# Attention of the first block: products with the values on column halves, transposed, and the division moved to the gate

## The chip, the cores and the metric

The kernel runs on one core of a Trainium2 chip. The metric is the device time of one execution in microseconds. The profile and the trace are of one further execution.

## The reference, cut to what matters

Two transformer blocks run one after the other over 256 tokens of width 1024. The first has two layers. Each mixes four branches of width 256 (attention, a convolution, a Fourier mix, a gated unit), multiplies them by a gate and projects the result out:

```
s = jnp.einsum("bqhd,bkhd->bhqk", q, k) * scale
pr = jax.nn.softmax(s, axis=-1)
attn = jnp.einsum("bhqk,bkhd->bqhd", pr, v)
...
y = jnp.concatenate([attn, conv, four, sgu], axis=-1) * jax.nn.silu(hp[..., GATE_OFF:])
return y @ p["w_out"]
```

The attention has four heads with values of width 64. In layer 0 the 256 tokens of `x` attend to 512 keys (x and context), and the 256 context tokens to the 256 context keys. In layer 1 only `x` has queries. The second block has two layers of feed-forward, token mixer, feed-forward; it reads the first block's output.

## The kernel before

Tokens are tiled by 128: tiles 0 and 1 are `x`, 2 and 3 the context. All products that need it are made in three passes: each float32 weight tile is streamed by SyncE (SP) into a `raw` buffer (`Stream.fetch`, L330), ScalarE (ACT) casts it to `whi`, VectorE (DVE) subtracts to get `wlo`, and TensorE (PE) multiplies high and low parts. `raw` has few slots, shared with the chunks `ada` of the matrix from which shift, scale and gate come. DVE multiplies each such chunk with the conditioning vector and sums it (`adaj`). So a DMA starts when DVE has let a buffer go, and PE's next weights wait for DMA, ACT and DVE in turn.

The order of each engine's instructions is fixed when the program is built: a planner in Python (`Sched`) keeps a clock per engine, adds an estimated cost per operation (`act` L216, `dve` L221, `mm` L230, `transpose` L234), and runs side jobs (`spawn`, generators that yield the time or the event they wait for) when they fall due. All instructions thus show the planner's lines, and their names tell them apart.

`First.attend` (L1621) handles one tile and one layer. For each head: scores `sc` on PE, the row maximum `mx` on DVE, `p` = exp on ACT with the row sums in `den`, transposes `tpp` of `p` in blocks of 128 keys, a copy to `pT` on ACT, the reciprocal `rd` on DVE. Then one matmul per key block, with `pT` as the 128x128 weights and 128 columns of `V` moving, which are two heads:

```
S.mm(ch, 0.218, av[:, :P], pT[:, j * P:(j + 1) * P],
     v[:, 2 * c:2 * c + 2, :].rearrange("p h d -> p (h d)"), start=j == 0, stop=j == nb - 1)
S.act(ch, 64, "mul", o[:, h * 64:(h + 1) * 64], av[:, b * 64:(b + 1) * 64], rd[:, h:h + 1], x=0.09)
```

Half of each result is not used. ACT divides the other half by the row sum into `att`. A tile has 4 key blocks (tiles 0 and 1) or 2 (tiles 2 and 3), so 16 or 8 such matmuls.

`put` (L1307) joins a branch and its gate. Whichever comes first is written to `y`, the second multiplies it on DVE. Branch 0 is the attention. For four of six tiles the attention came first and ACT copies it (`y<-att`), and the gate comes as a factor `fac`; for two the gate came first. Then `y_out` transposes `y` on PE (`tpy`), ACT makes the high part of `yT` and DVE the low part, and the output product `yo` uses them. The rest that the prediction names: `acc` (the convolution's 31 taps on DVE), `tpc<-acc` (its result transposed back), `ln` (its layernorm), `tpc<-ln` and `pw` (its pointwise product).

Of the kernel before, what the change touches and what calls it, by code (L numbers as in the profile page):

```python
# [8 lines left out]
F32 = mybir.dt.float32  # L9
F32R = mybir.dt.float32r  # L10
I32 = mybir.dt.int32
AF = mybir.ActivationFunctionType
ALU = mybir.AluOpType
PSUM = bass.MemoryType.PSUM
P = 128
# [135 lines left out]
class Event:  # L151
    def __init__(self):
        self.at = None
# [805 lines left out]
class Layer:  # L959


    def __init__(self):
        self.F, self.V, self.kT, self.qT, self.sgm, self.y, self.yT = {}, {}, {}, {}, {}, {}, {}


class First:
# [337 lines left out]
        S.act(ch, 256, "activation", z, src, AF.Identity, scale=r, bias=b, x=0.15)  # L1304
        return z

    def put(self, t, b, ch, emit=None, val=None):  # L1307

        S, l = self.S, self.l[t]
        L, key = self.L[l], (l, t, b)  # L1310
        T, i = (4, t) if l == 0 else (2, t % 2)
        if b not in L.y:
            L.y[b] = self.s4([P, T, 256], f"y{b}")
        dst = L.y[b][:, i, :]
        if key not in self.ystate:
            self.ystate[key] = ch
            if emit:
                emit(dst)
            else:
                S.act(ch, 256, "copy", dst, val)  # L1320
            return
        if emit:
            val = self.w2([P, 256], "fac")
            emit(val)
        ch.t = max(ch.t, self.ystate[key].t)
        S.dve(ch, 256, "tensor_tensor", dst, dst, val, op=ALU.mult)
        S.spawn(self.y_out(t, b, ch))

    def part(self, l, b, n):
        return self.L[l].yT[b][n] if l == 0 else self.L[l].yT[b][:, n]  # L1330

    def y_out(self, t, b, ch):
        S = self.S
        yield ch
        l = self.l[t]
        T, i = (4, t) if l == 0 else (2, t % 2)
        if b not in self.L[l].yT:
            self.L[l].yT[b] = [self.s4([P, 2, T, P], f"yT{b}{n}", F32R) for n in range(2)] if l == 0 else \
                self.s4([P, 2, 2, T, P], f"yT{b}", F32R)
        hi, lo = (self.part(l, b, n)[:, :, i, :] for n in range(2))  # L1340
        tp = self.psum("tp", "tpy")
        for c in range(2):
            self.tr(ch, tp[:, c * P:(c + 1) * P], self.L[l].y[b][:, i, c * P:(c + 1) * P])
        src = tp[:, :256].rearrange("p (c t) -> p c t", c=2)
        S.act(ch, 256, "copy", hi, src)
        S.dve(ch, 256, "tensor_sub", lo, src, hi.bitcast(F32))
        S.done(self.L[l].yev[t][b], ch)
# [273 lines left out]
    def attend(self, t, l):  # L1621

        S, L = self.S, self.L[l]
        s, i = divmod(t, 2)
        keys = (0, 1) if s == 0 else (1,)
        yield L.ev["mla", t]
        for k in keys:
            for j in range(2):
                yield L.ev["mla", 2 * k + j]
        nk = 256 * len(keys)  # L1630
        nb = nk // P
        den = self.small.tile([P, 4], F32, tag="den1", name="den1", bufs=4)
        rd = self.small.tile([P, 4], F32, tag="rd1", name="rd1", bufs=4)
        o = self.w2([P, 256], "att")
        for h in range(4):
            ps = self.psum("ps", "sc1")
            ch = S.chain()
            for n, k in enumerate(keys):
                S.mm(ch, 0.432, ps[:, n * 256:(n + 1) * 256], L.qT[s][:, h, i * P:(i + 1) * P], L.kT[k][:, h, :],
                     start=True, stop=True)  # L1640
            mx = self.small.tile([P, 1], F32, tag="mx1", name="mx1", bufs=4)
            S.dve(ch, nk, "tensor_reduce", mx, ps[:, :nk], axis=mybir.AxisListType.X, op=ALU.max, negate=True)
            p = self.w2([P, 512], "p1")
            S.act(ch, nk, "activation", p[:, :nk], ps[:, :nk], AF.Exp, bias=mx, accum_out=den[:, h:h + 1], x=0.19)
            yield ch
            tp = self.psum("tp", "tpp1")
            for j in range(nb):
                self.tr(ch, tp[:, j * P:(j + 1) * P], p[:, j * P:(j + 1) * P])
            pT = self.w2([P, 512], "pT1")
            S.act(ch, nk, "copy", pT[:, :nk], tp[:, :nk])  # L1650
            S.dve(Chain(ch.t), 16, "reciprocal", rd[:, h:h + 1], den[:, h:h + 1])
            yield ch
            av = self.psum("tp", "av1")
            c, b = divmod(h, 2)
            for j in range(nb):
                v = L.V[2 * keys[j // 2] + j % 2]
                S.mm(ch, 0.218, av[:, :P], pT[:, j * P:(j + 1) * P],
                     v[:, 2 * c:2 * c + 2, :].rearrange("p h d -> p (h d)"), start=j == 0, stop=j == nb - 1)
            S.act(ch, 64, "mul", o[:, h * 64:(h + 1) * 64], av[:, b * 64:(b + 1) * 64], rd[:, h:h + 1], x=0.09)
        self.put(t, 0, ch, val=o)  # L1660


    def weight(self, t):
# [33 lines left out]
    def begin(self, l):  # L1697

        if l in self.L:
            return  # L1700
        L = self.L[l] = Layer()
        L.c = self.layer_consts(l)
        L.ev = {(n, t): Event() for t in range(4) for n in ("glu", "mla", "sgu", "four")}
        L.yev = {t: [Event() for _ in range(4)] for t in range(4)}
        streams = (0, 1) if l == 0 else (0,)
        S = self.S
        S.spawn(self.conv(l, streams))
        for s in streams:
            S.spawn(self.fourier(l, s))
        for s in streams[::-1]:  # L1710
            S.spawn(self.attends(s, l))
# [234 lines left out]
```

## Time and profile before

| | |
|---|---|
| time, median of 3 runs | 1448.17 us (1447.13 to 1448.21) |
| profiled execution | 1447.77 us |
| its span, first to last instruction | 1446.0 us |
| mean granted TensorE clock | 0.996 of full |
| busy share of the span | PE 97%, DVE 69%, ACT 53%, POOL 2% |

The page gives each engine's busy time, a table of the span in 40 slices and the chain of work that ended last. The trace behind it gives each instruction's start, duration, and what ended the idle time before it. The first block fills the span to about 440 us, the second the rest. A float32 matmul of the program leaves two records on PE, and two weight loads on the load path (PEld).

### The profile page before, as it was taken

The numbers are of one execution on the slowest core, as the hardware profiler recorded it, in microseconds if no ns is written. First come the engines' busy times: TensorE is split into PE (matmuls) and PEld (weight loads), VectorE is DVE, ScalarE is ACT, GpSimd is POOL, SyncE is SP. The second block draws the span as 40 slices with busy tenths as digits, with TensorE's granted clock in tenths as the row PEclk, the third lists the DMA queues.
The fourth block names the chain that finished last, engine by engine and source line by source line (L and its number), as shares of the span: only waits on it lengthen the run. The fifth ranks groups of instructions, "written<-read, shape, count | busy, mean of one in ns | idle before, by whom it ended". The sixth has DMA issues, their size and how long they took to land.

```text
span 1446.0 us, 19092 instructions
## 1 busy us (share of the span) xinstructions
PE 1403.1 (97%) x6766; PEld 1134.5 (78%) x6766; DVE 1002.7 (69%) x2175; ACT 765.8 (53%) x1348; POOL 30.0 (2%) x46
## 2 busy tenths in 40 slices
PE   7999997999999999999999999999999999999997
PEld 4778886777877888777878888788887778788886
DVE  4899978779787555587886555765555878865554
ACT  4465533576565444567655444554445676554442
POOL 1000000000000000000000000000000000000000
PEclk9999999999999999999999999999999999999999
DMA  8751455333456555653446566566566534466551
GB/s 304 238 172 59 128 192 162 123 124 121 159 189 209 186 188 188 190 186 121 139 139 204 189 180 186 173 193 187 188 189 189 182 125 134 143 200 186 185 186 58
DMA packets 69088, 245.64 MB, mean 170 GB/s; under 512 B 7841, under 2 KB 8097, under 8 KB 68865
## 3 DMA queue, kind: packets, MB, share of 16 engines
q1 hardware_dynamic: 66384, 235.11, 51.1%
q0 software_dynamic: 2176, 8.79, 1.8%
q8 instruction: 53, 0.87, 0.2%
q10 hardware_dynamic: 432, 0.53, 0.1%
q14 instruction: 43, 0.34, 0.1%
HBM read 243.35 MB, written 1.05 MB: 169 GB/s over the span
## 4 chain that ended last, share of the span: by engine, by line
PE 79%; DVE 11%; DMA 4%; ACT 3%; issue 2%; SPq 0%; DVEq 0%; ACTq 0%
PE u L230 37%; PE y L230 18%; PE m L230 9%; DMA raw<-in_wst_dram 3%; PE yo L230 3%; DVE adaj L221 2%; DVE wlo L221 2%; PE av L230 2%; PE tpg L234 2%; DVE acc L221 1%; ACT whi L216 1%; PE tpp L234 1%; DMA ada<-in_adan_dram 1%; PE sc L230 1%; ACT f L216 1%
## 5 line engine op out<-in xcount | busy, mean ns | idle before, releaser
L221 DVE TENSOR_TENSOR wlo<-raw,whi 128x1024 fp32r<-128x1024 f32 (+1 forms) x380 | 459.2, 1211 | 341.8 <-ACT whi L216 339.4
L216 ACT CAST whi<-raw 128x1024 fp32r<-128x1024 f32 (+1 forms) x380 | 395.3, 1042 | 386.7 <-PE u L230 228.5
L230 PE MATMUL u<-whi,h_hi 128*128 128x512 f32 x704 | 281.2, 400 | 1.1 <-ACT h_hi L216 1.1
L230 PE MATMUL u<-whi,h_lo 128*128 128x512 f32 x704 | 275.0, 391 | 0.6 <-DVE h_lo L221 0.6
L230 PE MATMUL u<-wlo,h_hi 128*128 128x512 f32 x704 | 275.5, 392 | 0.0
L230 PE MATMUL y<-whi,g 128*128 128x512 f32 x704 | 218.3, 390 | 0.5 <-ACT g L216 0.5
L230 PEld LDWEIGHTS y<-whi,g 128*128 128x128 f32 x704 | 132.0, 188 | 28.8 <-ACT g L216 0.8
L230 PEld LDWEIGHTS u<-wlo,h_hi 128*128 128x128 f32 x704 | 132.1, 188 | 27.7
L230 PEld LDWEIGHTS u<-whi,h_lo 128*128 128x128 f32 x704 | 132.5, 188 | 27.1 <-DVE h_lo L221 2.5
L230 PEld LDWEIGHTS u<-whi,h_hi 128*128 128x128 f32 x704 | 132.2, 188 | 26.4 <-ACT h_hi L216 1.7
L230 PE MATMUL y<-wlo,g 128*128 128x512 f32 x352 | 137.3, 390 | 0.0
L230 PE MATMUL u<-whi,hhi 128*128 128x512 f32 (+2 forms) x256 | 98.7, 388 | 0.4 <-ACT whi L216 0.3
L221 DVE CUSTOM_DVE_ANT_0 adaj<-ada,cbc 128x1024 bf16<-128x1024 f32 x76 | 90.6, 1221 | 8.7 <-DMA ada<-in_ada_dram 8.6
L230 PE MATMUL u<-wlo,hhi 128*128 128x512 f32 (+2 forms) x256 | 94.4, 372 | 0.4 <-DVE wlo L221 0.4
L230 PE MATMUL u<-whi,hlo 128*128 128x512 f32 (+2 forms) x256 | 94.8, 372 | 0.0
L230 PE MATMUL m<-whi,h_hi 128*128 128x512 f32 x192 | 79.0, 415 | 0.4 <-ACT h_hi L216 0.4
L230 PEld LDWEIGHTS y<-wlo,g 128*128 128x128 f32 x352 | 66.1, 188 | 14.3
L230 PE MATMUL m<-wlo,h_hi 128*128 128x512 f32 x192 | 75.5, 395 | 0.0
L230 PE MATMUL m<-whi,h_lo 128*128 128x512 f32 x192 | 75.3, 394 | 0.0
L221 DVE SCALAR_TENSOR_TENSOR acc<-glu,cw,acc 128x512 f32<-128x512 f32 (+1 forms) x120 | 70.8, 613 | 0.0
L230 PEld LDWEIGHTS u<-whi,hhi 128*128 128x128 f32 x256 | 48.2, 189 | 8.3 <-issue 1.9
L230 PEld LDWEIGHTS u<-wlo,hhi 128*128 128x128 f32 x256 | 48.2, 188 | 8.0 <-DVE wlo L221 1.2
(294 smaller groups left out, 1961.6 us busy)
## 6 DMA issues: line engine op xcount, KB each, us to landing
raw<-in_wst_dram SPq DMA_DIRECT2D x376, 512.0 KB, 3.6
ada<-in_ada_dram SPq DMA_DIRECT2D x42, 512.0 KB, 4.3
grow<-in_rows_dram POOLq DMA_DIRECT2D x10, 512.0 KB, 5.1
raw<-in_wst_dram SPq DMA_DIRECT2D x8, 416.0 KB, 3.1
ada<-in_adan_dram SPq DMA_DIRECT2D x6, 512.0 KB, 5.3
raw<-in_wst_dram SPq DMA_DIRECT2D x8, 256.0 KB, 2.8
tab<-in_tab_dram POOLq DMA_DIRECT2D x1, 1536.0 KB, 8.4
x<-in_x_dram SPq DMA_DIRECT2D x2, 512.0 KB, 5.4
```

The source lines that it names most:

```text
L216: ins = getattr(self.nc.scalar, fn)(*a, **k)
L221: ins = getattr(self.nc.vector, fn)(*a, **k)
L230: self.nc.tensor.matmul(*a, **k)
L234: self.nc.tensor.transpose(out, in_, ident)
```

## The change

Two heads are now handled together. After the probabilities of a pair, each matmul has the values of one head as weights (64 columns) and `pT` moving. The heads of a pair write to the two halves of the output's partitions, so the result comes out transposed, and nothing of it is unused. There are two matmuls per key block and pair, 16 or 8 per tile as before. ACT copies a pair's 128x128 result to `oT` without dividing it.

The gate of branch 0 is always written first (`put` has lost its other path) and sets an event `g0`. A new job `att_out` waits for it and for the attention, multiplies the gate by `rd` on DVE, transposes the gate on PE, multiplies `oT` by the transposed gate on DVE (`attg`), and makes the high and low part of `yT` from that.

```diff
-            else:
-                S.act(ch, 256, "copy", dst, val)
+            emit(dst)
+            if b == 0:
+                S.done(L.ev["g0", t], ch)
             return
...
         nb = nk // P
...
-        o = self.w2([P, 256], "att")
+        if L.oT is None:
+            L.oT = self.s4([P, 4 if l == 0 else 2, 2, P], "oT")
+        o = L.oT[:, t if l == 0 else i]
+        pTs = []
         for h in range(4):
...
+            pTs.append(pT)
+            if h % 2 == 0:
+                continue
+
+            c = h // 2
             av = self.psum("tp", "av1")
-            c, b = divmod(h, 2)
             for j in range(nb):
                 v = L.V[2 * keys[j // 2] + j % 2]
-                S.mm(ch, 0.218, av[:, :P], pT[:, j * P:(j + 1) * P],
-                     v[:, 2 * c:2 * c + 2, :].rearrange("p h d -> p (h d)"), start=j == 0, stop=j == nb - 1)
-            S.act(ch, 64, "mul", o[:, h * 64:(h + 1) * 64], av[:, b * 64:(b + 1) * 64], rd[:, h:h + 1], x=0.09)
-        self.put(t, 0, ch, val=o)
+                for b in range(2):
+                    S.mm(ch, 0.104, av[b * 64:(b + 1) * 64, :P], v[:, 2 * c + b, :], pTs[b][:, j * P:(j + 1) * P],
+                         start=j == 0, stop=j == nb - 1)
+            S.act(ch, P, "copy", o[:, c, :], av[:, :P])
+            pTs = []
+        S.spawn(self.att_out(t, l, rd, o, ch))
+
+    def att_out(self, t, l, rd, o, ch):
+
+        S = self.S
+        yield self.L[l].ev["g0", t]
+        yield ch
+        i = t if l == 0 else t % 2
+        g = self.L[l].y[0][:, i, :]
+        cg = S.chain(ch)
+        gv = g.rearrange("p (h d) -> p h d", h=4)
+        S.dve(cg, 256, "tensor_tensor", gv, gv, rd.unsqueeze(2).to_broadcast([P, 4, 64]), op=ALU.mult)
+        yield cg
+        hi, lo = self.y_parts(t, l, 0)
+        tp = self.psum("tp", "tpy")
+        for c in range(2):
+            self.tr(cg, tp[:, c * P:(c + 1) * P], g[:, c * P:(c + 1) * P])
+        f = self.w2([P, 2, P], "attg")
+        S.dve(cg, 256, "tensor_tensor", f, o, tp[:, :256].rearrange("p (c t) -> p c t", c=2), op=ALU.mult)
+        S.act(cg, 256, "copy", hi, f)
+        S.dve(cg, 256, "tensor_sub", lo, f, hi.bitcast(F32))
+        S.done(self.L[l].yev[t][0], cg)
```

`y_parts` is the allocation of `yT`, taken out of `y_out`. Nothing else differs in the program's text. As costs and due times change, the planner puts other work elsewhere in the first block; the second block's order stays as it was. In all, ACT has 12 copies `oT` in place of 24 `att` and 4 `y<-att`, and two more loads of its function table; DVE has 6 `y*rd` and 6 `attg` in place of 2 `y<-y,att` and 4 `y<-y,fac`.

The first place is on PE, at the first products of layer 0's attention: two key blocks for a context tile, four for an `x` tile (`V` are the values by key block). Before:

```order
L230 MATMUL av_1209<-V_943,pT_1194 128x128
L230 MATMUL av_1209<-V_1016,pT_1194 128x128
L230 MATMUL sc_1213<-T_980,T_987 128x256
L230 MATMUL av_1219<-V_893,pT_1202 128x128
L230 MATMUL av_1219<-V_918,pT_1202 128x128
L230 MATMUL av_1219<-V_943,pT_1202 128x128
L230 MATMUL av_1219<-V_1016,pT_1202 128x128
L230 MATMUL sc_1225<-T_997,T_1004 128x256
```

Now:

```order
L230 MATMUL av_1260<-pT_1193,V_943 64x128
L230 MATMUL sc_1266<-T_980,T_987 128x256
L230 MATMUL av_1260<-pT_1247,V_943 64x128
L230 MATMUL av_1260<-pT_1193,V_1016 64x128
L230 MATMUL av_1260<-pT_1247,V_1016 64x128
L234 MATMUL tpp_1272<-ident,p_1224 128x128 x4
L230 MATMUL av_1292<-pT_1201,V_893 64x128
L230 MATMUL sc_1302<-T_997,T_1004 128x256
L230 MATMUL sc_1302<-T_980,T_1004 128x256
L230 MATMUL av_1292<-pT_1277,V_893 64x128
L230 MATMUL av_1292<-pT_1201,V_918 64x128
L230 MATMUL av_1292<-pT_1277,V_918 64x128
```

A pair's products alternate between its two `pT`, and score rows have come between the first of them and the rest.

The second place is on DVE, at the end of layer 0's attention. Before, from the last weights of 512 columns on:

```order
L221 TENSOR_TENSOR wlo_2044<-raw_1827,whi_2043 128x512
L221 TENSOR_TENSOR y_1407<-y_1407,att 128x256
L221 TENSOR_TENSOR yT_2035<-tpy,yT_2034 128x2x128
L221 TENSOR_TENSOR wlo_2058<-raw_1855,whi_2057 128x512
L221 TENSOR_TENSOR wlo_2070<-raw_2041,whi_2069 128x512
L221 TENSOR_TENSOR y_1407<-y_1407,fac 128x256
L221 ISA adaj,ada_115<-ada_16_1940,cbc_117 128x1024
```

Now, up to the same weights' first two:

```order
L221 SCALAR_TENSOR_TENSOR acc<-glu,cw_100,acc 128x512
L221 TENSOR_TENSOR y_1882<-y_1882,rd_1096 128x256
L221 SCALAR_TENSOR_TENSOR acc<-glu,cw_100,acc 128x512 x3
L221 RECIPROCAL rd_1551<-den_1550 128x1
L221 SCALAR_TENSOR_TENSOR acc<-glu,cw_100,acc 128x512
L221 TENSOR_TENSOR y_1882<-y_1882,rd_1551 128x256
L221 SCALAR_TENSOR_TENSOR acc<-glu,cw_100,acc 128x512 x2
L221 TENSOR_TENSOR wlo_1987<-raw_1756,whi_1986 128x512
L221 TENSOR_TENSOR wlo_2000<-raw_1774,whi_1999 128x512
L221 TENSOR_TENSOR attg<-oT,tpy 128x256
L221 TENSOR_TENSOR y_1882<-y_1882,rd_1490 128x256
L221 SCALAR_TENSOR_TENSOR acc<-glu,cw_100,acc 128x512
```

Eight `acc` that ran earlier before now stand around these weights, with the products of gate and `rd` between them.

The third place is on PE, at the end of layer 0, where the convolution's four results are transposed for their layernorms. Before:

```order
L234 MATMUL tpc<-ident,acc 128x128 x2
L230 MATMUL yo_2466<-whi_2259,yT_2281 128x512
L234 MATMUL tpc<-ident,acc 128x128 x2
L230 MATMUL yo_2466<-wlo_2260,yT_2280 128x512
L230 MATMUL yo_2466<-whi_2259,yT_2280 128x512
L230 MATMUL yo_2466<-whi_2259,yT_2281 128x512
L230 MATMUL yo_2466<-wlo_2260,yT_2280 128x512
L234 MATMUL tpc_2473<-ident,ln 128x128 x2
L234 MATMUL tpc_2491<-ident,ln 128x128 x2
L230 MATMUL pw<-pw,cs 128x256 x4
```

Now:

```order
L230 MATMUL yo_2353<-whi_2236,yT_2256 128x512
L230 MATMUL yo_2353<-wlo_2237,yT_2255 128x512
L234 MATMUL tpc<-ident,acc 128x128 x8
L234 MATMUL tpc_2486<-ident,ln 128x128 x2
L234 MATMUL tpc_2498<-ident,ln 128x128 x2
L230 MATMUL pw<-pw,cs 128x256 x2
L234 MATMUL tpc_2510<-ident,ln 128x128 x2
L230 MATMUL pw<-pw,cs 128x256 x2
```

Before, two more pairs `tpc<-acc` stood 35 and 18 rows ahead of the two shown; now all four pairs come together behind the last `yo`.

## Rows read from the trace of the kernel before

**Rows 1.** The page's chain that ended last, share by engine.
```profile
PE 79%; DVE 11%; DMA 4%; ACT 3%; issue 2%; SPq 0%; DVEq 0%; ACTq 0%
```
**Rows 2.** Busy us per stretch: length, each engine, granted clock, DMA share, GB/s.
```profile
110.00:120.00 10.00, 9.86 (x58) 8.03 (x58) 9.85 (x27) 4.27 (x13) 0.00 (x0) 1.00 0.01 2
...
220.00:230.00 10.00, 8.13 (x34) 6.74 (x35) 9.10 (x18) 1.59 (x5) 0.00 (x0) 0.83 0.80 226
...
240.00:250.00 10.00, 5.87 (x22) 3.99 (x20) 6.62 (x31) 4.36 (x9) 0.00 (x0) 0.83 0.50 158
```
**Rows 3.** Timeline, PE: start, duration, operation, idle before and its releaser.
```profile
221.87 1.09 PE L234 MATMUL tpy<-ident,y 128*128 128x128 f32 x4 [3.54 <-DVE y L221]
...
245.14 1.14 PE L234 MATMUL tpc<-ident,ln 128*128 128x128 f32 x4 [4.03 <-ACT ln L216]
```
**Rows 4.** Pieces of the chain: start, us, what; x counts records.
```profile
113.83 0.66 DVE acc L221
...
117.69 0.89 PE av L230 x8
...
383.82 5.77 DMA raw<-in_wst_dram
...
399.69 0.91 PE av L230 x8
...
412.41 4.11 PE yo L230 x18
...
441.31 3.73 PE u L230 x15
```
**Rows 5.** All records of tile `av`: min/median/max ns, first and last start.
```profile
L230 PE MATMUL av<-V,pT x160: 270/275/377, 116.7 to 408.7; 128*128 128x128 f32 x160
L230 PEld LDWEIGHTS av<-z,v x72: 132/137/137, 700.7 to 1227.6; 128*64 128x64 f32 x72
L230 PE MATMUL av<-z,v x72: 272/273/323, 700.7 to 1227.7; 128*64 128x128 f32 x72
```
**Rows 6.** Timeline, PE, two stretches of the second block's attention.
```profile
700.72 0.88 PE L230 MATMUL av<-z,v 128*64 128x128 f32 x12
...
702.18 0.33 PE L234 MATMUL tpp<-ident,scb_s 128*128 128x128 f32 x1
...
1225.87 0.39 PE L230 MATMUL y<-whi,m_lo 128*128 128x512 f32 x1
1226.10 0.39 PE L230 MATMUL y<-wlo,m_hi 128*128 128x512 f32 x1
1226.42 1.53 PE L230 MATMUL av<-z,v 128*64 128x128 f32 x24
...
1229.19 0.48 PE L230 MATMUL scb<-kT,qz 128*128 128x256 f32 x1
```
**Rows 7.** Groups on ACT, 0 to 460 us: busy us, mean ns, idle before.
```profile
L216 ACT ACT_TABLE_LOAD x9 | 11.5, 1283 | 1.9 <-PEq L1937 1.2 <-DVE mx L221 0.6
L216 ACT ACTIVATE att<-av,rd 128x64 f32<-128x64 f32 x24 | 7.6, 316 | 14.1 <-PE av L230 14.0
```
**Rows 8.** Timeline, DVE, 201 to 222 us.
```profile
206.48 0.69 DVE L221 TENSOR_TENSOR wlo<-raw,whi 128x512 fp32r<-128x512 f32 x1 [3.57 <-ACT whi L216]
207.09 0.42 DVE L221 TENSOR_TENSOR y<-y,fac 128x256 f32<-128x256 f32 x1
...
216.71 1.23 DVE L221 CUSTOM_DVE_ANT_0 adaj<-ada,cbc 128x1024 bf16<-128x1024 f32 x1 [2.75 <-DMA ada<-in_ada_dram]
...
221.30 0.76 DVE L221 TENSOR_TENSOR y<-y,fac 128x256 f32<-128x256 f32 x2
```
**Rows 9.** Timeline, DVE and ACT, the second pair of layernorms.
```profile
239.94 0.76 DVE L221 BATCH_NORM_STATS2 bn<-tpc 128x6 f32<-128x256 f32 x2
...
243.98 0.16 DVE L221 SCALAR_TENSOR_TENSOR lnb<-mv,rs_y 128x1 f32<-128x1 f32 x1
...
244.53 1.01 ACT L216 ACTIVATE ln<-tpc,lnb,rs_y 128x256 f32<-128x256 f32 x2
```

More of the change, by code (lines that the diff above doesn't have):

```diff
@@ L963, in __init__ @@
         self.F, self.V, self.kT, self.qT, self.sgm, self.y, self.yT = {}, {}, {}, {}, {}, {}, {}
+        self.oT = None
 class First:
@@ L1305, in layernorm, with put @@
         return z
-    def put(self, t, b, ch, emit=None, val=None):
+    def put(self, t, b, ch, emit):
         S, l = self.S, self.l[t]
@@ L1316, in put @@
             self.ystate[key] = ch
-            if emit:
-                emit(dst)
-            else:
-                S.act(ch, 256, "copy", dst, val)
+            emit(dst)
+            if b == 0:
+                S.done(L.ev["g0", t], ch)
             return
-        if emit:
-            val = self.w2([P, 256], "fac")
-            emit(val)
+        val = self.w2([P, 256], "fac")
+        emit(val)
         ch.t = max(ch.t, self.ystate[key].t)
@@ L1327, in put, with y_parts @@
         S.spawn(self.y_out(t, b, ch))
+    def y_parts(self, t, l, b):
+        T, i = (4, t) if l == 0 else (2, t % 2)
+        if b not in self.L[l].yT:
+            self.L[l].yT[b] = [self.s4([P, 2, T, P], f"yT{b}{n}", F32R) for n in range(2)] if l == 0 else \
+                self.s4([P, 2, 2, T, P], f"yT{b}", F32R)
+        return [self.part(l, b, n)[:, :, i, :] for n in range(2)]
     def part(self, l, b, n):
@@ L1336, in y_out @@
         T, i = (4, t) if l == 0 else (2, t % 2)
[L1337 to L1340, printed above, removed]
+        hi, lo = self.y_parts(t, l, b)
         tp = self.psum("tp", "tpy")
@@ L1702, in begin @@
         L.c = self.layer_consts(l)
-        L.ev = {(n, t): Event() for t in range(4) for n in ("glu", "mla", "sgu", "four")}
+        L.ev = {(n, t): Event() for t in range(4) for n in ("glu", "mla", "sgu", "four", "g0")}
         L.yev = {t: [Event() for _ in range(4)] for t in range(4)}
```

## Prediction

> **What bounds the kernel now.** I read the chain that ended last first. TensorE (PE) holds 79% of it, VectorE (DVE) 11%, DMA 4% [rows 1]. The kernel is a matmul kernel with stretches in which something else decides, and the change touches only the first block, which ends near 440 us. So the second view is the busy time by stretches [rows 2]. While layer 0's attention runs (110 to 120 us) PE and DVE are both full, 9.86 and 9.85 of 10 us. At 220 to 230 us PE is busy for only 8.13, at 240 to 250 for 5.87, and the granted clock falls to 0.83 of full there, so part of each stretch runs at the lower of the two levels, 1.2 GHz. The third view is PE's own timeline. It waits 3.54 us for DVE's `y` at 218.3 to 221.9 and 4.03 us for ScalarE's `ln` at 241.1 to 245.1 [rows 3]. A microsecond saved on PE ahead of those two waits counts only if DVE and ACT come earlier too. That question is most of this prediction.
>
> **The products themselves.** Before, one product of probabilities and values (a 128x128 program matmul, two records each) takes a quarter of 0.89 us: 0.2225 us [rows 4]. There are 160 records [rows 5], so 80 program matmuls: 48 in layer 0 (two tiles with 16, two with 8) and 32 in layer 1. They cost 10.68 and 7.12 us of PE. They lie on the chain in both layers, between other PE work (two of the places stand in [rows 4]).
>
> The change keeps 80 program matmuls, but each has 64 columns. The trace has that very form in the second block: `av<-z,v`, weights 128*64 [rows 5]. Its price comes from two stretches [rows 6]. In one, 24 records (12 of `av<-z,v`, 12 of `av<-pTA,v`, together 12 program matmuls) begin at 700.72 and the next operation at 702.18: 1.46 us. In the other, 48 records (24 program matmuls) begin at 1226.42, the next operation at 1229.19: 2.77 us. Twelve more cost 1.31 us, so one costs **0.109 us**, half of 0.2225: the two column halves do overlap. What is left, 1.46 - 1.31 = 0.15 us, belongs to the stretch. On entering it there is more: the rows before 1226.42 step by 0.23 us (1225.87, 1226.10), the first 64-column row comes 0.32 us after the last of them, 0.09 more. So **every unbroken stretch of 64-column matmuls costs a fixed 0.24 us**.
>
> How many stretches there are is read from the new order, of which the first fence ahead shows two heads: a lone product, a score or other rows, then the rest. Layer 0 has 12 stretches (of 1, 3, 1, 7, 1, 3, 8, 1, 3, 8, 4 and 8), layer 1 five (1, 7, 8, 8, 8). A stretch of odd length leaves one product without a partner on the other half; I charge 0.11 us for it, the other half of 0.2225. There are eight in layer 0 and two in layer 1.
>
> - Layer 0: 48 x 0.109 + 12 x 0.24 + 8 x 0.11 = 5.23 + 2.88 + 0.88 = 8.99 against 10.68: **-1.7 us**. If odd lengths cost nothing, -2.6; if the fixed part vanished too, -5.4.
> - Layer 1: 32 x 0.109 + 5 x 0.24 + 2 x 0.11 = 3.49 + 1.20 + 0.22 = 4.91 against 7.12: **-2.2 us**. The same bounds: -2.4 and -3.6.
>
> So PE's work falls by 3.9 us, at best by 9.0.
>
> A rule speaks against it. The 64-column weight loads take 0.137 us each [rows 5], and 48 records with as many loads fit into 2.77 us, 0.058 each, so most of every load is hidden [rows 6]. The Trainium skill, page "TensorE: Matmul & The Clock Gate", section "Part 3: Packing small matmuls — row/col tiling", says that a weight load overlaps running matmuls only when its row group differs, which two column halves do not offer; by that 160 loads would stand bare at 0.137 us, an estimated 21.9 us against the 17.8 of before, a loss of 4.1. The measured rows decide, and the sum takes 0.109.
>
> **What goes and comes on the other engines.** ACT loses 24 `att` (7.6 us busy) [rows 7] and four copies, and gains 12 copies of 128x128, priced near a 64-column `att`, some 4 us. It gains two activation table loads at 1.28 us each [rows 7], since the gate is now always written before the probabilities' factor. ACT is busy for less than half of these stretches [rows 2] and holds PE up behind the attention only with `ln` and `whi`, which the change leaves alone [rows 3, 9], so I cost this at nothing; bare, the two loads would cost 2.6 us. DVE gains six `y*rd` and six `attg` and loses six products of the same 128x256 form: six more. Two of that form in a row take 0.76 us where one shows 0.42 [rows 8], so each adds 0.34, six 2.0. Four of them are in layer 0 (1.4 us) and fall where DVE is nearly full. The division used to lie on ACT; that it moves to a full DVE is the price of the change.
>
> **What DVE does with it in layer 0.** To the row `y<-y,fac x2` at 221.30, for which PE waits 3.54 us, DVE's work is the same to within those additions, as convolution rows have moved. But before, DVE itself waits for 3.57 us at 202.9 to 206.5 (for `whi`, behind a weight DMA) and 2.75 us at 214.0 to 216.7 (for an `ada` DMA) [rows 8]. In the new order (second fence) eight convolution `acc` (0.66 us on the chain [rows 4], 5.3 us in all) are still to be done there: they fill the first gap. I take DVE to reach that row 4 to 6 us earlier, and PE, which now has 20 output matmuls (`yo`) ahead of the transposes where it had four, no longer waits there. That is the gain.
>
> It is given back one step later, at the convolution's end (third fence). Before, the four pairs of `tpc<-acc` transposes are spread among the `yo`, so two of the four layernorm chains run beside them. Now all eight stand behind the last `yo`. Only two `tp` buffers hold them, so the chains come in two rounds. One round is 239.94 to 244.14 on DVE (with one `wlo` inside) and 0.50 us on ACT before PE goes on: about 5 us [rows 9]. I put the last `yo` at 234 to 235 (241.1 before, less the 3.5 of wait, less 1.7, less the transposes that moved behind it), the first chains' end near 240 and the second's near 244.5, against 245.14. The two `attg` products of the x tiles, and so their `yT`, stand in the new DVE order behind a `wlo` and two `adaj` (1.23 us each [rows 8]), which may make PE wait for up to 3 us before the attention's own `yo`. So I take **-1.0 us** at the end of layer 0, out of -6 to +5.
>
> **Layer 1.** From 260 to 350 us the order is the same, the shift is carried. Behind that PE holds most of the chain up to a weight DMA, which decides from 383.82 for 5.77 us, and most of it again from the `av` at 399.69 to the `yo` that end at 416.5 [rows 4]. Five stretches lie mostly on PE's parts. Of 2.2 us I count 2.0: **-2.0**. The second block's order is the same and it is bound by PE and weights; nothing is won or lost.
>
> Sum: -1.0 - 2.0 = -3.0 us against the profiled execution's own 1447.77 (span 1446.0 and 1.8 around it): 1444.8. The median of the runs stands 0.40 us above that execution: **1445.2 us**.
>
> **Rivals.**
> - *Everything is carried.* Layer 0's two PE waits shrink as DVE comes earlier, and the two rounds of layernorm overlap with late `yo`: -5 to -6 there, -2 to -3 in layer 1: about -8, 1440. For it: DVE's gaps of 6.3 us are waits, not work. Against it: the second round is serial.
> - *The waits take it all.* DVE and the DMAs hold the ends of both layers; PE arrives earlier and waits longer: 0 within 1 us, 1448. For it: in both layers the chain leaves PE for a DMA just behind the attention [rows 4, 8].
> - *The lump costs more than it hides.* If DVE does not reach the `fac` rows at least 3 us earlier, PE's last `yo` stays past 239, and two rounds of 4.5 to 5 us follow where one wait of 4.03 stood: +5, of which layer 1 gives 1 to 2 back, and PE's clock falls during the wait, as it does now: +3.5, 1451.7. For it: DVE is full and has 1.4 us more work. Against it: the gaps of [rows 8] have more room than that.
>
> That the halves do not run together, so that nothing is saved, is excluded by [rows 6].
>
> **How the numbers follow.** Forecast 0.40, everything carried 0.17, the waits take it all 0.23, the lump 0.20. A measurement of this kernel can tell about 0.2%, 2.9 us, from no change; that is 1445.3, right at the forecast. So "faster" has the whole of the second case and somewhat over half of the first: 0.42. "Same" has the rest of the first, all of the third, minus a little: 0.39. "Slower" (over 1451.1) has most of the lump: 0.19. The range reaches from the carried case to the lump's, half a microsecond beyond each: 1439.5 to 1452.2, which leaves out about half of either's spread; the likeliest case's own is 1443 to 1447.
>
> **What would show it.** The 64-column `av` rows at 0.109 us a program matmul and some 0.24 per stretch; PE's wait for `y` near 222 gone or under 1 us; DVE's gap before 206 filled by `acc`; `y<-y,fac x2` at 215 to 217; a PE wait before `tpc<-ln` split in two, its end between 243 and 246; the first `u` of the second block 2 to 4 us before 441.31 [rows 4]. Wrong would be: `y<-y,fac x2` after 219, or 64-column rows above 0.15 us, or PE waits before the output matmuls of the attention of more than 3 us.

## The result, and the profile after

The changed kernel takes 1457.61 us (median of 4 runs, 1456.1 to 1457.86), the kernel before 1447.65 us in the same comparison: a ratio of **1.0062, 95% interval 1.005 to 1.0075**. By the ratio the change costs 9 us (the medians differ by 10). Forecast were 1445.2 us, 1439.5 to 1452.2, with 0.19 for slower.

The profiled execution has a span of 1456.1 us, 10.1 more than before. Three places divide it: the first output product `yo`, the first `tpgate` row (layer 0's products are then nearly done) and the last `yo` of layer 1. They stand in the records by tile, whose last columns are the first and last start. Before:

```profile
L230 PE MATMUL yo<-whi,yT x160: 387/389/775, 217.2 to 420.7; 128*128 128x512 f32 x160
L230 PE MATMUL yo<-w,yT x48: 387/392/578, 388.7 to 425.5; 128*128 128x512 f32 x48
...
L234 PE MATMUL tpgate<-ident,ada x24: 270/272/277, 255.5 to 412.1; 128*128 128x128 f32 x24
```

After:

```profile
L230 PE MATMUL yo<-whi,yT x160: 387/390/629, 216.7 to 432.1; 128*128 128x512 f32 x160
L230 PE MATMUL yo<-w,yT x48: 387/390/482, 391.9 to 436.9; 128*128 128x512 f32 x48
...
L234 PE MATMUL tpgate<-ident,ada x24: 270/273/276, 261.6 to 421.5; 128*128 128x128 f32 x24
```

So PE reaches its first `yo` 0.5 us earlier, the `tpgate` row 6.1 us later and the last `yo` 11.4 us later. Layer 0's end loses 6.6 us, layer 1 another 5.3. The second block gives 1.3 back. These numbers say where the delay shows; what a repair in one place would bring is another question, which the experiments take up.

PE's waits between 100 and 440 us, the longest first (total, times, longest):

```profile
PE tpc L234 <- ACT ln L216: 8.1, 2, 4.9
PE tpp L234 <- ACT ln L216: 5.3, 1, 5.3
PE yo L230 <- DVE wlo L221: 4.5, 1, 4.5
PE dft L230 <- ACT dftz L216: 1.7, 2, 0.9
```

Before there was one wait of 4.03 us for `ln` and one of 3.54 for `y` [rows 3]; the rest were 1.6 and less. Now both layers wait for a layernorm at the convolution's tail, layer 0 twice. The timeline of PE shows the places (start, duration, idle before and its releaser):

```profile
223.14 0.79 PE L230 MATMUL yo<-wlo,yT 128*128 128x512 f32 x1 [4.48 <-DVE wlo L221]
223.74 1.05 PE L230 MATMUL yo<-whi,yT 128*128 128x512 f32 x2
224.59 1.05 PE L230 MATMUL yo<-wlo,yT 128*128 128x512 f32 x2
...
246.80 1.14 PE L234 MATMUL tpc<-ident,acc 128*128 128x128 f32 x4 [4.86 <-ACT ln L216]
251.21 1.14 PE L234 MATMUL tpc<-ident,ln 128*128 128x128 f32 x4 [3.26 <-ACT ln L216]
...
408.90 1.11 PE L234 MATMUL tpp<-ident,p 128*128 128x128 f32 x4 [5.30 <-ACT ln L216]
```

The two `yo` at 223.74 take 0.85 us until the next pair, 0.43 each, where one takes 0.23 at full clock: PE works at half pace behind the wait. The stretches show the granted clock (the last column but two):

```profile
220.00:230.00 10.00, 6.86 (x21) 5.39 (x22) 9.10 (x20) 1.94 (x6) 0.00 (x0) 0.66 0.65 196
240.00:250.00 10.00, 3.09 (x15) 1.99 (x13) 7.79 (x46) 3.11 (x4) 0.00 (x0) 0.79 0.50 160
250.00:260.00 10.00, 8.69 (x34) 6.59 (x35) 4.75 (x15) 5.25 (x13) 0.00 (x0) 0.70 0.02 6
400.00:410.00 10.00, 4.70 (x23) 3.76 (x23) 8.06 (x33) 4.16 (x7) 0.00 (x0) 0.81 0.78 268
410.00:420.00 10.00, 8.73 (x45) 6.14 (x44) 3.90 (x10) 5.44 (x15) 0.00 (x0) 0.68 0.01 2
```

Before, only two stretches between 100 and 440 us were below 1.00, at 0.83 [rows 2]. The mean granted clock fell from 0.996 to 0.988.

The products themselves do what was forecast. One stretch of eight of them (16 records), with the row behind it:

```profile
151.35 1.09 PE L230 MATMUL av<-pT,V 128*64 128x128 f32 x16
152.37 1.13 PE L230 MATMUL sc<-T,T 128*128 128x256 f32 x4
```

1.02 us for eight is 8 x 0.109 + 0.15, to the hundredth what [rows 6] gave. So the loss is not in the price of the changed products.

### The profile page after: what moved, and what is told of

Read it like the earlier page. It is cut to its first block, busy times and chain, and to the rows that moved or that the text cites. A ratio compares the mean times of both kernels' runs of the same rounds, so it can differ in the third digit from the quotient of the medians.

```text
span 1456.1 us, 19062 instructions
## 1 busy us (share of the span) xinstructions
PE 1405.8 (97%) x6766; PEld 1129.6 (78%) x6766; DVE 1004.2 (69%) x2181; ACT 765.3 (53%) x1334; POOL 30.1 (2%) x46
## 4 chain that ended last, share of the span: by engine, by line
PE 75%; DVE 14%; DMA 5%; ACT 4%; issue 2%; SPq 0%; DVEq 0%; ACTq 0%
PE u L230 34%; PE y L230 18%; PE m L230 9%; DMA raw<-in_wst_dram 3%; PE yo L230 3%; DVE wlo L221 2%; DVE acc L221 2%; DVE adaj L221 2%; DMA ada<-in_ada_dram 2%; PE tpg L234 1%; ACT whi L216 1%; DVE rs_t L221 1%; PE av L230 1%; PE tpp L234 1%; ACT f L216 1%
```

## The experiments

The theories, as they stood before the runs. **A**: the loss is the order, in which the convolution's tail comes behind all other work of PE, so that its layernorms are waited for in the open. **B**: the division and gating on DVE cost more than they save. After the first four runs a third was added. **C**: part of the loss is the clock. After the next four came **D**: DVE, not PE, sets the end of layer 0, so that what PE saves becomes waiting.

"Cover" below is the PE work in the order between a convolution result's transposes and those of its layernorm, estimated from the printed order at 0.23 us for a product and 0.11 for a transpose: 0.9, 0.9, 1.1, 1.3 us for the four results of layer 0 and 2.7 twice in layer 1 in the changed kernel, against 9.6, 5.9, 2.5, 2.2 and 12.8 twice before.

**One number of the planner, in the changed kernel.**

```diff
-CONV = 3
+CONV = 5
```

> The changed kernel with one number of the planner altered: the convolution may run up to 5 us (not 3) ahead of DVE's planned backlog, so its taps end earlier in the order. Between the transposes of the convolution's result and those of its layernorm PE then has 8.7, 8.7, 5.2, 5.0 us of planned work in layer 0 and 9.1 in layer 1, where the changed kernel has 0.9 to 1.3 and 2.7 and the kernel before 9.6, 5.9, 2.5, 2.2 and 12.8. Theory A (lost cover: the loss is the convolution's tail, which the new order puts behind all of PE's other work): the two waits of 8.1 us at 241 to 251 and the one of 5.3 at 403 to 409 shrink to some 4 together, time 1445 to 1450. Theory B (the division and gating on DVE make attention's end late): the time stays at 1455 to 1459.

Measured: 1459.09 us, ratio 1.0075 (1.0057 to 1.0093): for the whole, just over the upper end of B's range and far from A's. By layer it splits: the first `tpgate` row is at 258.1 us (261.6 in the changed kernel, 255.5 before), so more than half of layer 0's loss came back with the cover:

```profile
L234 PE MATMUL tpgate<-ident,ada x24: 270/272/275, 258.1 to 418.1; 128*128 128x128 f32 x24
```

But from there to the last `yo` layer 1 takes 178.2 us, against 175.3 and 170.0: the convolution, let run ahead, pushed layer 1's attention back (its first product comes 6 us later than in the changed kernel). That cover bought with DVE's time is paid for elsewhere is a reading of these rows, not shown by them: the run with the pairing undone, further down, loses as much in layer 1 without it.

**The price of a product as the planner sees it.**

```diff
-                    S.mm(ch, 0.104, av[b * 64:(b + 1) * 64, :P], v[:, 2 * c + b, :], pTs[b][:, j * P:(j + 1) * P],
+                    S.mm(ch, 0.14, av[b * 64:(b + 1) * 64, :P], v[:, 2 * c + b, :], pTs[b][:, j * P:(j + 1) * P],
```

> The changed kernel with the planner's price of a 64-column matmul set to 0.14 us, near what the trace shows with its fixed part, instead of 0.104; the work is the same. The order then gives layer 1 its cover back (11.9 and 7.3 us between the convolution's transposes and the layernorms') but not layer 0 (2.3, 2.3, 1.1, 1.3). Theory A: layer 1's 5 us come back, layer 0's 6 stay: 1451 to 1454. Theory B: 1455 to 1459.

Measured: 1455.24 us, ratio 1.0043 (1.0028 to 1.0059), about 1 us over A's range and at the lower edge of B's, so the total does not tell them apart. The split is as A has it: the first `tpgate` row at 262.0, nothing back, and from it to the last `yo` 171.8 us, 3.5 of layer 1's 5.3 back. PE, DVE, ACT and POOL carry out as many instructions as in the changed kernel.

**No division.**

```diff
-        S.dve(cg, 256, "tensor_tensor", gv, gv, rd.unsqueeze(2).to_broadcast([P, 4, 64]), op=ALU.mult)
+        S.issue("dve", cg, 0.07 + 256 * 0.00104)
```

> The changed kernel without the division: the six products of gate and reciprocal row sum on DVE are left out, so the attention's part of the output is not divided; the planner still counts their time, so the order is nearly that of the changed kernel, and the convolution's tail has the same cover as there. Theory A: DVE gains 2 us of work at most, 1455.5 to 1458. Theory B: 1448 to 1452.

Measured: 1458.49 us, ratio 1.0068 (1.0053 to 1.0083), the changed kernel's 1.0062 within the intervals, half a microsecond over A's range and 6 over B's. The division's six products are not what costs 9 us; B falls as far as they go.

**The same setting in the kernel before.**

```diff
-CONV = 3
+CONV = 5
```

> The kernel before with the same number of the planner altered from 3 to 5. Its convolution tail then lies ahead of all output matmuls in layer 0 (cover 12.8, 12.8, 2.0, 2.2 us) and has 8.0 and 13.5 in layer 1. Theory A: the kernel before had most of its cover already; between 1444 and 1450, and by the difference to the first run the change is worth -3 to +2 at equal setting. Theory B: this stays 8 or more below the first run.

Measured: 1467.38 us, ratio 1.0129 (1.0114 to 1.0145): 19 us worse, far outside what either theory said. With the convolution ahead of everything the attention comes late (first `yo` at 251.6 us instead of 217.2). The old setting was fitted to the old program, and more cover is not better in itself. That made the plain form of A too simple: it is the whole order that counts, and the tail is one place where it shows.

**All of the change's operations in the old order.** This is the run that decides. The planner is charged the old operations; the new ones are issued beside it.

```diff
+            pTs.append(pT)
+            for j in range(nb):
+                S.issue("pe", ch, 0.218)
+            S.issue("act", ch, 0.095 + 64 * 0.00083 + 0.09)
+            if h % 2 == 0:
+                continue
...
+                for b in range(2):
+                    S.nc.tensor.matmul(av[b * 64:(b + 1) * 64, :P], v[:, 2 * c + b, :], pTs[b][:, j * P:(j + 1) * P],
+                                       start=j == 0, stop=j == nb - 1)
+            S.nc.scalar.copy(o[:, c, :], av[:, :P])
...
+            f = self.w2([P, 2, P], "attg")
+            S.nc.vector.tensor_tensor(f, o, src, op=ALU.mult)
```

> All operations of the change (64-column products by head pairs, undivided copies, division on the gate, attg) in the planner's order of the kernel before: the planner is charged the old operations' costs and sees neither the new price nor the new steps. The convolution's tail keeps the cover of the kernel before (9.4, 5.7, 2.5, 2.2 us in layer 0, 11.7 and 11.9 in layer 1). Theory A (the loss is all order): 1443.5 to 1449, at or under the kernel before, layer 0's first tpgate row at 253 to 257 us. Theory B (the new operations cost more than they save, wherever they stand): 1452 or more.

Measured: 1449.71 us against 1449.3 in the same comparison, **ratio 1.0002 (0.9992 to 1.0012)**. That is 0.7 us over A's range and 2 under B's. The new operations cost nothing where the old order very nearly holds (of PE's 6462 records other than `av`, some 50 stand elsewhere than before, in the changed kernel some 370): the 9 us are the order. They also gain nothing, though PE's saving is there: its first `yo` comes at 215.4 us, 1.8 earlier than before. It is lost at the next row of PE, and DVE shows why:

```profile
222.65 1.09 PE L234 MATMUL tpy<-ident,y 128*128 128x128 f32 x4 [5.23 <-DVE y L221]
...
219.79 1.23 DVE L221 CUSTOM_DVE_ANT_0 adaj<-ada,cbc 128x1024 bf16<-128x1024 f32 x1 [2.42 <-DMA ada<-in_ada_dram]
```

The wait that was 3.54 us [rows 3] is 5.23, and ends 0.8 us later. DVE's added products are not what holds it up there: the two transfers of `ada` ahead of that row start 0.9 us earlier than before, but the second takes 7.29 us from issue to landing instead of 4.59, and DVE waits for it. (This profile is of an execution 2 us above the median, with the first `tpgate` row at 257.8, just outside A's 253 to 257; its later rows are not used.)

**Idle work for PE in the waits.**

```diff
+        if l == 0 and t == 1:
+            for _ in range(40):
+                S.nc.tensor.transpose(tp[:, 256:384], self.id, self.id)
...
+        if t == 0:
+            for _ in range((28, 40)[l]):
+                S.nc.tensor.transpose(tp[:, :P], self.id, self.id)
```

> The changed kernel in its own order with idle work for PE in its three waits at the convolutions' tails: 40 transposes of the identity after the second result's transposes in layer 0, 28 before the first layernorm's transposes there, 40 at the same place in layer 1; their results are overwritten or never read. Theory C (part of the loss is the clock: it falls to 1.2 GHz after these waits, and PE runs at half pace for some us behind each): the granted clock stays at 1.00 in 250 to 260 and 410 to 420 us, where the changed kernel has 0.70 and 0.68, and the time falls by 2 to 5 us, to 1452.5 to 1455.5. If the clock doesn't matter, the time stays or rises by up to 3.

Measured: 1464.53 us, ratio 1.0105 (1.009 to 1.0121): slower than the changed kernel, and the clock still fell:

```profile
250.00:260.00 10.00, 8.09 (x41) 7.53 (x42) 3.32 (x23) 3.09 (x7) 0.00 (x0) 0.66 0.07 29
...
410.00:420.00 10.00, 5.22 (x33) 4.83 (x34) 4.98 (x27) 2.61 (x7) 0.00 (x0) 0.83 0.42 133
```

The filler missed the waits. In layer 0 a wait of 3.38 us was left behind the first 40 transposes, and the 28 stood behind that wait. In layer 1 the wait of 4.83 us came ahead of the filler, at the `tpp` rows, and the 40 transposes then took another 5.3 us of the path. So what the clock alone costs is not settled by a run. What the traces give is half pace on the rows behind a wait.

**The pairing undone.**

```diff
-            for j in range(nb):
-                v = L.V[2 * keys[j // 2] + j % 2]
-                for b in range(2):
+            for b in range(2):
+                for j in range(nb):
+                    v = L.V[2 * keys[j // 2] + j % 2]
```

> The changed kernel with the two heads' products one after the other instead of alternating: first all blocks of one head on the left half, then all of the other. The halves no longer find a partner, so a product should take 0.22 us and PE loses what the change saved, 3.9 to 4.5 us; the order is otherwise the changed kernel's. If PE's saving reaches the end of the layers: 1460 to 1462. If DVE and the convolution's tail hold the ends (theory A): 1457 to 1459.

Measured: 1458.23 us, ratio 1.0061 (1.0047 to 1.0075), the changed kernel's own. The same eight products now take 1.51 us instead of 1.02 (start to the row behind):

```profile
151.91 1.58 PE L230 MATMUL av<-pT,V 128*64 128x128 f32 x16
153.42 1.13 PE L230 MATMUL sc<-T,T 128*128 128x256 f32 x4
...
221.95 0.50 PE L230 MATMUL yo<-wlo,yT 128*128 128x512 f32 x1 [1.50 <-DVE wlo L221]
...
L234 PE MATMUL tpgate<-ident,ada x24: 270/272/281, 258.4 to 421.5; 128*128 128x128 f32 x24
```

That is 0.19 a product, not 0.22 as expected; over 80 products some 4 to 5 us of PE are given away if the others do as these eight, and the time does not move. But it stays the same as a sum of two differences. PE comes to its first `yo` 1.7 us later (218.4), waits 1.50 us for `wlo` instead of 4.48, keeps a granted clock of 1.00 in 220 to 230 us where it was 0.66, and has its first `tpgate` row 3.2 us *earlier*. In layer 0 of this profile, then, what PE saves only becomes waiting, and the clock falls behind the longer wait. From there to the last `yo` (436.9) layer 1 takes 3.2 us longer.

Whether those 3.2 us are the slower products is not settled. In the changed kernel and the runs with `CONV = 5`, without the division and without the pairing, the first `tpgate` row lies at 261.6, 258.1, 260.0 and 258.4, and the last `yo` at 436.9, 436.3, 436.7 and 436.9: in all of them layer 1 swallows what layer 0 wins. So layer 0's 6.6 us are no sum that a repair there alone would give back.

**The kernel before in another order.**

```diff
-                S.mm(ch, 0.218, av[:, :P], pT[:, j * P:(j + 1) * P],
+                S.mm(ch, 0.2, av[:, :P], pT[:, j * P:(j + 1) * P],
```

> The kernel before with the planner's price of a product set to 0.200 instead of 0.218 and nothing else: the same work in another order, in which the first two convolution results of layer 0 are transposed 24 and 10 output matmuls later (cover 3.6, 3.6, 1.1, 1.3 us instead of 9.6, 5.9, 2.5, 2.2); layer 1 keeps its cover. Theory A: layer 0 loses 2 to 6 us without any new work, 1450 to 1454. If order at the tail is not the cause: 1446 to 1449.

Measured: 1459.21 us, **ratio 1.0068 (1.0054 to 1.0082)**. An untouched program loses as much as the change did, from one number of the planner. That is 5 us over A's range, and A's place for it was wrong: 7.8 us are gone already at the first `yo` (225.0 us instead of 217.2). The tail then waits in two rounds, as in the changed kernel:

```profile
249.02 1.15 PE L234 MATMUL tpc<-ident,acc 128*128 128x128 f32 x4 [3.80 <-ACT ln L216]
255.06 1.15 PE L234 MATMUL tpc<-ident,ln 128*128 128x128 f32 x4 [4.89 <-ACT ln L216]
```

**The changed kernel with the old price.**

```diff
-                    S.mm(ch, 0.104, av[b * 64:(b + 1) * 64, :P], v[:, 2 * c + b, :], pTs[b][:, j * P:(j + 1) * P],
+                    S.mm(ch, 0.218, av[b * 64:(b + 1) * 64, :P], v[:, 2 * c + b, :], pTs[b][:, j * P:(j + 1) * P],
```

> The changed kernel, planned by itself, with the planner's price of a product put back to 0.218 us, the old one, and nothing else. Cover of the convolution's results in layer 0 is 9.2, 4.8, 1.1, 1.3 us (the kernel before 9.6, 5.9, 2.5, 2.2; the changed one 0.9, 0.9, 1.1, 1.3), in layer 1 11.9 and 12.1. Theory A (order at the tail): 1448 to 1452, most of the loss gone, layer 1 from its first tpgate to the last output product within 3 us of the kernel before. If the tail's cover is not what counts: 1455 or more.

Measured: 1448.63 us against 1449.35, **ratio 1.0001 (0.9993 to 1.001)**. One number brings all of the loss back, with the work as the change has it. It does so without bringing back the old order: some 360 of PE's 6462 records other than `av` stand elsewhere than before, about as many as in the changed kernel. Its waits are back to one of about 4 us at layer 0's tail (total, times, longest), the first `tpgate` row is at 255.5 and the last `yo` at 426.2:

```profile
PE tpc L234 <- ACT ln L216: 5.2, 4, 3.7
PE dft L230 <- ACT dftz L216: 1.6, 3, 0.8
```

**The division on POOL, old order.**

```diff
-        S.dve(ch, 256, "tensor_tensor", gv, gv, rd.unsqueeze(2).to_broadcast([P, 4, 64]), op=ALU.mult)
+        S.issue("dve", ch, 0.07 + 256 * 0.00104)
+        S.nc.gpsimd.tensor_tensor(gv, gv, rd.unsqueeze(2).to_broadcast([P, 4, 64]), op=ALU.mult)
```

> The change's operations in the order of the kernel before, as in the run before this one, with the six products of gate and reciprocal row sum moved from DVE to POOL, which is idle there. Theory D (DVE, not PE, sets the end of layer 0, so PE's 4 us only become waiting, and DVE's added work costs about as much as it is): 1 to 2 us below the run with all of it on DVE, if a POOL product takes under 2 us each; else the same.

Measured: 1450.03 us against 1449.35, ratio 1.0001 (0.9989 to 1.0012): no gain that can be measured, where D had 1 to 2 us. A product takes 0.87 us on POOL, twice DVE's 0.42 (group of POOL: busy us, mean ns, idle before):

```profile
L1339 POOL TENSOR_TENSOR y<-y,rd 128x256 f32<-128x256 f32 x6 | 5.2, 870 | 243.3 <-ACT y L216 159.4 <-DVE y L221 59.0 <-DVE rd L221 24.9
```

The run also shows how far one profile can be leaned on. Its order is all but that of the other run in the old order, yet its first `tpgate` row lies at 253.0 us, there at 257.8; the profiled executions were 4 us under and 2 us over their medians. The splits by place above rest on one profile a kernel.

**Without `attg`, old order.**

```diff
-            f = self.w2([P, 2, P], "attg")
-            S.nc.vector.tensor_tensor(f, o, src, op=ALU.mult)
-            src = f
+            pass
```

> The change's operations in the order of the kernel before, without the six products attg of attention and transposed gate: the attention's result is left out of the output and the divided gate is used alone; DVE then has as many products there as in the kernel before, PE keeps its saving. Theory D: DVE reaches the fac rows at the kernel before's 221 us or 1 earlier, and the time is -0.5 to -2.5 us against the kernel before. If PE's saving is carried wherever DVE isn't loaded more: -3 to -4.5 us.

Measured: 1447.31 us against 1449.35, ratio 0.9989 (0.9981 to 0.9998), -1.6 us with an interval from -2.8 to -0.3. That is within D's range and under the -3 of a saving that is carried whole. But not as D had it: DVE reaches its `fac` rows at 218.03 us, 3.3 earlier than before, not up to 1. And more than DVE's load differs: a step between PE's transposes and `yT` is gone, the second `ada` transfer takes 5.36 us, and the order has moved (the eight `yo` that stood ahead of the wait for `y` come behind it, the first at 218.8). What of the 1.6 us is DVE's load is not shown.

**Old price and POOL together**, the attempt at a version that beats both.

```diff
-        S.dve(cg, 256, "tensor_tensor", gv, gv, rd.unsqueeze(2).to_broadcast([P, 4, 64]), op=ALU.mult)
+        S.pool(cg, 0.87, "tensor_tensor", gv, gv, rd.unsqueeze(2).to_broadcast([P, 4, 64]), op=ALU.mult)
```

(with the price 0.218 of the run above)

> The changed kernel with the old price of 0.218 us and with the six products of gate and reciprocal row sum on POOL, planned there at 0.87 us each as measured in an earlier run. The convolution's tail has the cover of the kernel before (9.2, 5.5, 2.5, 2.2 us; 12.1, 12.1). Theories A and D together: DVE is loaded as in the kernel before plus 0.7 us in layer 0, the tail is covered, PE's saving may show in part: 1446 to 1449, between -3 and 0 us against the kernel before. If POOL's longer product or its wait delays the attention's end: 1449 to 1452.

Measured: 1449.54 us against 1449.23, ratio 1.0005 (0.9996 to 1.0014): not the 1446 to 1449 of A and D together. No version tried here that does all of the work beats the kernel before.

## Why the prediction was wrong

**The products' price: right.** 0.109 us a product and 0.15 inside a stretch were measured again in place (1.02 us for eight). That the halves overlap, against the weight-load rule of the Trainium skill that the prediction quotes, is confirmed: those 1.02 us hold 16 loads, which bare at 0.137 us [rows 5] would take 2.2. The first `yo` came 1.8 us earlier in the old order, where -1.7 was forecast, and 0.5 in the new one, where `dft` rows wait 0.9 us more.

**"I take DVE to reach that row 4 to 6 us earlier": this step failed first.** DVE reached `y<-y,fac x2` at 221.20, against 221.30 [rows 8]. The gap before 206 was filled by `acc`, as said. But DVE let the next `ada` buffers go only 1.4 us earlier, so their two transfers started at 209.66 and 211.95 instead of 211.09 and 213.38. The first landed 1.9 us earlier, the second 0.9 *later*, at 218.88: it took 6.93 us where it had taken 4.59. Two new waits for `ada` opened in place of the old ones.

```profile
206.86 1.29 DVE L221 TENSOR_TENSOR wlo<-raw,whi 128x512 fp32r<-128x512 f32 x2
...
214.82 1.22 DVE L221 CUSTOM_DVE_ANT_0 adaj<-ada,cbc 128x1024 bf16<-128x1024 f32 x1 [2.49 <-DMA ada<-in_ada_dram]
...
218.90 1.23 DVE L221 CUSTOM_DVE_ANT_0 adaj<-ada,cbc 128x1024 bf16<-128x1024 f32 x1 [1.71 <-DMA ada<-in_ada_dram]
...
221.20 0.76 DVE L221 TENSOR_TENSOR y<-y,fac 128x256 f32<-128x256 f32 x2
```

The prediction counted 6.3 us of waits as room that work could fill. It did not ask which DMA would be waited for next, when its buffer came free, and what would be in flight beside it. POOL copies the context tiles (`xc`, 512 KB each, like an `ada` chunk) when their buffer is free. Such a copy now started just ahead of the second `ada`; before, one ran beside the first, from 209.78. The queues of the changed kernel:

```profile
211.62 0.54 POOL L1770 DMA_DIRECT2D xc<-in_ctx_dram  x1 [169.57 <-PE tpy L234]
...
211.95 6.93 DMA ada<-in_ada_dram
```

From 210 to 220 us 304 GB/s were moved, 211 before. In the run with the old order an `xc` and a slow second `ada` (7.29 us) overlap too. That the copy is what slows the transfer is not shown: with the division on POOL they overlap as well, and `ada` takes 4.53.

So PE's wait did not go. It was to be under 1 us at the transposes of `y`; it is 4.48 us at the output product that needs the `wlo` behind that row, and layer 0's last `yo` before the convolution ends at 241.9 us, not at 234 to 235.

**The lump: the right rival, at too low a chance.** The condition that it named, that DVE does not come at least 3 us earlier, was met. It put the loss at the end of layer 0 at +5, and +6.6 was measured between the first `yo` and the first `tpgate` row. Two rounds of layernorm are there as described, 4.86 and 3.26 us of wait, and the granted clock is 0.79 and 0.70 in the two stretches around them. The sum took -1.0 because it rested on the step above.

**Layer 1: "of 2.2 us I count 2.0" failed altogether**, +5.3 instead of -2.0. The prediction priced the products there and did not read the order of that layer's tail, where the same thing had happened: the transposes of the convolution's result had moved back until six `yo` and four `sc` records were all that PE had before the next wait (cover 2.7 us instead of 12.8). On the chain, the layernorm of this tail is reached through two weight DMAs in a row, which stand ahead of it in the queues of ACT and DVE:

```profile
388.76 5.72 DMA raw<-in_wst_dram
394.50 1.06 ACT whi L216
395.58 1.24 DVE wlo L221
396.84 5.03 DMA raw<-in_wst_dram
401.89 1.06 ACT w L216
...
408.28 0.57 ACT ln L216
```

The one number that brings the cover back here, the price of 0.14, brings 3.5 us back. The lump, which had layer 1 give 1 to 2 us back, missed the total for the same reason.

**What was shown and what was not.** Shown: the loss is the order, since the new operations in nearly the old order cost 1.0002, one number in the planner undoes the loss, and another puts a loss of the same size, most of it at an earlier place, on the old program. Shown too: in the new order undoing PE's saving leaves the time as it is. By the profiles the saving only becomes waiting in layer 0; whether it does so in layer 1 is not shown. Not shown either: what eats the saving in the old order. D's answer, DVE's load, failed in the run on POOL, and the run without `attg`, which gains 1.6 us, changes more than the load. Read from the traces, not isolated: that the tails' lost cover is the part of the order that costs, how much of the 9 us is waiting, and how much is half pace behind the waits. Only argued: why the price of 0.218 does best. It is not the true one, and 0.14, which is nearer, does worse; that the other numbers of the planner were fitted to the timing of the old price is an inference.

## What to carry to other kernels

Where a planner sets the order, a change of a cost is two changes, and the second can be larger: run the new operations in the old order, and the old operations with a shifted price, before judging either. Read the new order at every tail for the work that covers it, in all layers, not only where the edit's own operations stand. Waiting time of an engine behind DMAs is not room: ask when the next transfer can start if it is filled, and what will then be in flight beside it. And a loss that shows in two places need not be two losses that can be won back one by one.

## What the runs showed of the hardware

Pairing within a stretch matters: alternating halves gave 1.02 us for eight 64-column products, one half after the other 1.51. That is less than the 1.78 of eight full products; why is not shown. Entering and leaving such a stretch costs: [rows 6] show 0.09 us on entry. The Trainium skill, page "TensorEngine Tiling (Array Packing)", section "Key Properties", says that a change of tiling mode drains the array; the trace agrees as far as that gap of 0.09 us goes. The 108 transposes of filler left the granted clock at 0.66 and 0.83 in the stretches where 1.00 had been expected; as they stood behind the waits or left part of them open, this does not show what filler within a wait would do. And one and the same transfer of 512 KB, the second `ada` ahead of the `fac` rows, took 4.59 us in the kernel before, 6.93 in the changed one, and 7.29 and 4.53 in two runs that differ by little more than the engine of the division: a DMA that an engine waits for has no fixed price.
